# A hybrid encoder block on one core: one more seven-product pair of k-tiles in ten blocks, an eighth load place, new step lists

## The chip, the core and the metric

The kernel runs on one core of one Trainium2 chip. The metric is the device time of one execution in microseconds (us); less is better. The core's engines are TensorE (PE, with PEld for its weight loads), VectorE (DVE), ScalarE (ACT), GpSimd (POOL) and SyncE (SP); SP issues nearly all loads, POOL issues those that add to what is in place.

## The reference

One layer of an encoder block on 256 tokens of width 2048, in float32. Cut to what matters here:

```
proj = rms_norm(x) @ w_in            # q/k/v of mixers A and B, q of C, three gates
merged = sum over A, B, C of  sigmoid(gate_i) * (mixer_i @ w_br_i)
x = x + merged @ w_o                 # 2048 x 2048
hf = rms_norm(x) @ w_ffn_in          # 2048 x 11264
x = x + (silu(hf[:, :5632]) * hf[:, 5632:]) @ w_ffn_out
```

Nearly all of the time is these matrix products: 256 rows of activations by weights that are read once.

## The kernel before, in words

**Products.** Each float32 operand is split into a high part and the rest, both in the format that TensorE reads at full rate. For a weight tile ACT writes the high part (`whi`, line 395) and DVE subtracts it to get the rest (`wlo`, line 405). A product of two tiles is then three matmuls: high by high, high by rest, rest by high. All of them are issued at line 77.

**Blocks.** From `merging` on (line 816) the work is a row of blocks. A block makes 256 tokens by two neighbouring groups of 512 output columns, over 16 k-tiles of 128 (12 in the last two blocks), taken two at a time as a pair `u`. `pair` (line 407) makes one block, by a list of steps written out by hand (the `STEPS` strings, lines 54 to 61). The list says for each pair whether it takes eight products or seven:

- `d` and `D`: a whole pair for the first and the second column group, four products each. So a pair in the plain way costs eight products (24 matmuls) and two loads, each split once.
- `f`, `g`, `h`, `p`, `q`: a pair by Strassen's scheme in Winograd's form, with seven products (21 matmuls). `fetch_both` (line 479) loads both column groups into two places, `b1` and `b2`, and has POOL issue a third load that adds the first group's first half to `b2` (line 483). `f` (`first`) splits `b1`: two products. `g` (`second`) makes the sums s2 and s3 on DVE (lines 504 and 505), splits `b2`: two products. `h` (`third`) makes the fourth sum, s2 + b1 (line 523), splits it: one product. `p` and `q` (`rest`) split s2 and s3 of two pairs at a time: one product for each pair. The activations' sums that the scheme needs, the forms, are made by `sums_of` (line 796) and `token_sums` (line 787).

In the lists, `h1` serves all seven-product pairs from 1 up to the next `h`. Two fourth sums stay in the two `b1` places until the `h` step, which splits them as two halves of 512 columns, by two instructions on ACT and two on DVE.

**What sets the order.** The steps of all blocks form one chain. `run` (line 576) lets the splits go up to four steps ahead of the products. Instructions on TensorE and SP keep the program's order, and so do the splits and sums on ACT and DVE that go through `follow`; the rest (the ends of blocks, transposes, gates) is placed between them. `whi` and `wlo` have four buffers each and a fifth for every fifth step (`halves`, line 385).

**Places.** Loads go into places (`free`, line 199; `load`, line 205), taken from the front of a list and put back at its end once split: six from the start and a seventh after the attention part (line 782). `pair` fetches a seven-product pair up to four steps before its `f` if more than four places are free, else at `f` itself (lines 560 to 564). A load into a place waits until the place's last reader is done, and SP's later loads stand behind it.

**The blocks in order.** The gate and branch blocks of `merging` (one gate block by `STEPS_GATE`, four by `STEPS`, branch products between them), two blocks by `w_o` (`STEPS_O`), then eleven blocks by `w_ffn_in` (the first by `STEPS_FFN`, the others by `STEPS_IN`) with, after the 4th, the 8th and the last, two blocks by `w_ffn_out` (`STEPS_OUT` and `STEPS_OUT2`, at the end twice `STEPS_LAST`).

Of the kernel before, what the change touches and what calls it, by code (L numbers as in the profile page):

```python
# [18 lines left out]
P = 128  # L19
# [31 lines left out]

STEPS = "d0 D0 f1 d4 g1 D4 f2 d5 g2 D5 h1 f3 d6 g3 h3 p0 p2 D6 q0 q2 d7 D7".split()
STEPS_GATE = "d0 D0 d4 D4 f1 d5 g1 D5 f2 g2 d6 h1 f3 g3 h3 p0 p2 D6 q0 q2 d7 D7".split()
STEPS_IN = "d0 D0 f1 d5 g1 D5 f2 g2 h1 f3 d6 g3 f4 g4 h3 p0 p2 D6 q0 q2 d7 D7".split()
STEPS_FFN = "d0 D0 d1 D1 d4 D4 f2 d5 g2 D5 f3 d6 g3 h2 p0 D6 q0 d7 D7".split()
STEPS_O = "d0 D0 d1 D1 f2 d4 g2 D4 f3 d5 g3 D5 h2 d6 p0 D6 q0 d7 D7".split()
STEPS_OUT = "d0 D0 d1 D1 d2 D2 f6 d3 g6 D3 f7 d4 g7 h6 p0 D4 q0 d5 D5".split()
STEPS_LAST = "d0 D0 f2 d1 g2 D1 f3 d4 g3 h2 p0 D4 q0 d5 D5".split()  # L60
STEPS_OUT2 = "d0 D0 f5 d1 g5 D1 f6 d2 g6 D2 h5 f7 d3 g7 h7 p0 p2 D3 q0 q2 d4 D4".split()


class InOrder:
# [37 lines left out]
def encoder_block(ctx: ExitStack, tc: tile.TileContext, a: dict, out: bass.AP):  # L102
# [93 lines left out]
            tick()  # L196

    spare = []
    free, place_of = [(rp, f"raw{i}") for i in range(6)], {}

    def release(raw):

# [204 lines left out]
    def pair(src, lhs, order, done, forms=None, operand=None, parts=None):  # L407
# [92 lines left out]
        def second(u):  # L500
            def ready():
                b1, b2 = held[u]
                s2, s3 = t2[:, those.index(u)], t3[:, those.index(u)]
                nc.follow(nc.vector.tensor_add(s2, b2[:, 0], b2[:, 1]))
                nc.follow(nc.vector.tensor_sub(s3, s2, b1[:, 0]))
                hi, lo = halves(b2)
                release(b2)

                def products():
                    mul("W", forms(u, 0), hi[:, 0], lo[:, 0])  # L510
                    mul("Z", forms(u, 2), hi[:, 1], lo[:, 1])
                    if left["W"] == 0:
                        copy(("B", 1), "W")
                return products
            return ready

        def third(u):
            us = [v for v in those if u <= v and not any(u < w <= v for w in fourths)]

            def ready():  # L520
                low_ones = [held.pop(v)[0] for v in us]
                for v, b1 in zip(us, low_ones):
                    nc.follow(nc.vector.tensor_add(b1[:, 1], t2[:, those.index(v)], b1[:, 1]))
                hi, lo = halves(*(b1[:, 1] for b1 in low_ones))
                for b1 in low_ones:
                    release(b1)

                def products():
                    for i, v in enumerate(us):
                        mul("V", at(2 * v + 1, 1), hi[:, i], lo[:, i])  # L530
                return products
            return ready
# [279 lines left out]
    def form_room(n, pool=None):  # L812
        tiles = [s8([P, 2, 2, 4, P], "forms", pool=pool) for _ in range((n + 1) // 2)]
        return [tiles[i // 2][:, i % 2] for i in range(2 * len(tiles))]

    def merging():
        forms = sums_of(xT, (1, 2, 3), form_room(3, tail))
        for b, (g0, k0, k1) in enumerate(((0, 0, 2), (8, 2, 6), (4, 6, 12))):
            for j in (0, 2) if b else (2,):
                sg = [None, None]  # L820

                def gates(c, r, sg=sg):
                    sg[c] = r
                    for t in range(T):
                        nc.scalar.activation(r[:, t], r[:, t], AF.Sigmoid, scale=r_x[:, 0, t:t + 1])

                def merge(c, r, j=j, b=b, sg=sg):
                    n0 = (j + c) * NC
                    for t in range(T):
                        nc.vector.tensor_mul(sg[c][:, t] if b else mg[t][:, n0:n0 + NC], r[t], sg[c][:, t])  # L830

                    def later():
                        yield 1
                        for t in range(T):
                            m = mg[t][:, n0:n0 + NC]
                            nc.vector.tensor_add(m, m, sg[c][:, t])
                        if b == 2:
                            to = s8([P, 2, 4, S], "mT", pool=tail)
                            mT.append(to)
                            yield 2  # L840
                            yield from transposed([mg[t][:, n0:n0 + NC] for t in range(T)],
                                                  lambda k, n: (to[:, 0, k:k + n], to[:, 1, k:k + n]))
                    if b:
                        start(urgent(later()))

                yield pair(block_pair(a["w_gate"], g0 + j), xT, STEPS if b else STEPS_GATE, gates, forms)
                yield pair(lambda u, c, j=j, k0=k0: a["w_br"][j + c][k0 // PK + u], lambda k, k0=k0: ol(k0 + k),
                           whole_k((k1 - k0) // 2), merge)

# [4 lines left out]
    def projecting():  # L854
# [2 lines left out]
            nc.sync.dma_start(out=x[t], in_=a["x"][t * P:(t + 1) * P, :])  # L857
        x1T.extend(s8([P, 2, 4, S], "x1T") for _ in range(4))
        mTl = lambda k: (mT[k // 4][:, 0, k % 4], mT[k // 4][:, 1, k % 4])
        oforms = sums_of(mTl, (2, 3), form_room(2))  # L860
        for n in (0, 2):
            def add(c, r, n=n):
                xc = [x[t][:, (n + c) * NC:(n + c + 1) * NC] for t in range(T)]
                for t in range(T):
                    nc.vector.tensor_add(xc[t], r[:, t], xc[t])

                def later():
                    yield 1
                    sq = s4([P, T, NC], "sq")
                    for t in range(T):  # L870
                        nc.scalar.activation(sq[:, t], xc[t], AF.Square, accum_out=ss1[:, t, n + c:n + c + 1])
                    yield 2
                    yield from transposed(xc, lambda k, m: (x1T[n + c][:, 0, k], x1T[n + c][:, 1, k]),
                                          lambda k: gT[:, 2, 4 * (n + c) + k:4 * (n + c) + k + 1], 2)
                    if n + c == 1:
                        room.extend(form_room(4) + [spare[0].tile([P, 2, 4, P], F32R, name="form")])
                        forms.append(by_pair((1, 2, 3, 4), room[:4]))
                        sums_of(x1l, (1, 2, 3), room[:3])
                    elif n + c == 2:
                        sums_of(x1l, (4,), room[3:4])  # L880
                    elif n + c == 3:
                        yield 2
                        ssr = small.tile([P, T], F32, name="ss", bufs=1)
                        nc.vector.tensor_reduce(ssr, ss1, axis=AX.X, op=ALU.add)
                        row_scale(ssr, r_f)
                start(urgent(later()))
            yield pair(block_pair(a["w_o"], n), mTl, STEPS_O, add, oforms)

# [5 lines left out]
    def feeding():  # L894
        for c0, c1 in ((0, 4), (4, 8), (8, KF // 4)):
# [25 lines left out]
                yield pair(lambda u, c, n=n: a["w_ffn"][n][2 * u + c], x1l, STEPS_IN if n else STEPS_FFN, hidden,  # L921
                           lambda u, f: forms[0](u, f))
            if last:
                pairs = STEPS_LAST, STEPS_LAST
                out_forms = by_pair((2, 3), late)
            else:
                pairs = STEPS_OUT, STEPS_OUT2
                sums_of(hTl, (5,), room[4:])
# [111 lines left out]
```

## Time and profile before

| | before |
|---|---|
| median of 3 runs | 1371.34 us (1371.25 to 1371.46) |
| the profiled execution's own time | 1371.87 us |
| its span, first to last instruction | 1370.0 us |
| TensorE clock granted | 1.000 |
| DVE busy | 1165.8 us (85%) |
| ACT busy | 848.6 us (62%) |
| POOL busy | 78.1 us (6%) |
| loads of a pair added to by POOL | 75 |

The profile page has the busy time of each engine, the span in 40 slices, and the chain of work that ended last, followed back from the end. The view of waits lists for each engine what it waited for: us in total, times, the longest. The windows view gives busy time by engine in chosen stretches, with the number of instructions in brackets.

### The profile page before, as it was taken

To read this page: it belongs to the slowest core of one execution; us is meant where nothing else is said; L and a number is where in the kernel's file an instruction comes from. 1 tells how busy PE (TensorE), PEld (TensorE's weight loads), DVE (VectorE), ACT (ScalarE), POOL (GpSimd) and SP (SyncE) were. 2 spreads that over 40 slices of the span, in tenths; PEclk is the share of its full clock that TensorE was granted. 3 is DMA by queue.
4 is the path that set the end of the run, shared out by engine and by line. 5 is a ranking of instruction groups with operands and counts; after the bars stand their busy time and mean duration, and the time that the engine had idled before them with its cause. 6 is when DMAs were issued, how large, how long until landed. Compare 5 with 4: busy or idle time off the path is not lost.

```text
span 1370.0 us, 17909 instructions
## 1 busy us (share of the span) xinstructions
PE 1362.6 (99%) x6219; PEld 1129.1 (82%) x6219; DVE 1165.8 (85%) x1646; ACT 848.6 (62%) x1158; POOL 78.1 (6%) x89
## 2 busy tenths in 40 slices
PE   9999999999999999999999999999999999999998
PEld 7888888888888888888888888887888888888887
DVE  6868877758878878878989998989899988999997
ACT  7777666646665564656666666555566664566663
POOL 0010000000000000000000000000010000010000
PEclk9999999999999999999999999999999999999999
DMA  9876455557776776765767776777787767677773
GB/s 367 328 241 204 144 160 161 175 172 226 211 240 194 213 238 196 275 195 177 221 200 238 228 220 200 218 238 213 215 244 224 230 202 229 209 236 230 224 223 109
DMA packets 90524, 296.78 MB, mean 217 GB/s; under 512 B 10241, under 2 KB 12801, under 8 KB 90177
## 3 DMA queue, kind: packets, MB, share of 16 engines
q1 hardware_dynamic: 79488, 275.94, 59.9%
q0 software_dynamic: 10800, 19.67, 8.7%
q8 instruction: 49, 0.80, 0.2%
q14 instruction: 43, 0.34, 0.1%
q10 hardware_dynamic: 144, 0.02, 0.0%
HBM read 292.71 MB, written 2.88 MB: 216 GB/s over the span
## 4 chain that ended last, share of the span: by engine, by line
PE 95%; DVE 3%; DMA 1%; issue 0%; ACT 0%; SPq 0%; DVEq 0%; ACTq 0%
PE mm L77 16%; PE mmZ L77 16%; PE mmV L77 16%; PE mmY L77 16%; PE mmQ L77 13%; PE mmX L77 11%; PE mmW L77 3%; DVE wlo L405 1%; PE tp L77 1%; PE sc L77 1%; PE o L77 1%; DMA raw<-in_w_ffn 1%; PE pT L77 1%; PE hT L77 0%; DMA raw<-in_w_mem 0%
## 5 line engine op out<-in xcount | busy, mean ns | idle before, releaser
L395 ACT ACTIVATE whi<-raw 128x1024 fp32r<-128x1024 f32 (+1 forms) x490 | 479.4, 991 | 370.2 <-PE mmV L77 98.3
L405 DVE TENSOR_TENSOR wlo<-raw,whi 128x1024 fp32r<-128x1024 f32 (+1 forms) x490 | 549.4, 1137 | 99.2 <-ACT whi L395 94.9
L77 PE MATMUL mm<-whi,xT 128*128 128x512 f32 x640 | 203.0, 393 | 0.0
L77 PEld LDWEIGHTS mm<-whi,xT 128*128 128x128 f32 x640 | 119.2, 188 | 24.3 <-issue 1.1
L131 DVE TENSOR_TENSOR wlo<-raw,whi 128x1024 fp32r<-128x1024 f32 x82 | 101.8, 1245 | 40.3 <-ACT whi L130 39.8
L77 PE MATMUL mm<-wlo,xT 128*128 128x512 f32 x320 | 125.3, 392 | 0.0
L130 ACT ACTIVATE whi<-raw 128x1024 fp32r<-128x1024 f32 x82 | 86.7, 1061 | 61.8 <-PE mm L77 45.7
L405 DVE TENSOR_TENSOR wlo<-t,whi 128x1024 fp32r<-128x1024 f32 x82 | 90.0, 1130 | 20.2 <-ACT whi L395 20.1
L77 PE MATMUL mmX<-whi,forms 128*128 128x512 f32 x292 | 97.7, 389 | 0.0
L77 PE MATMUL mmY<-whi,x1T 128*128 128x512 f32 x268 | 95.8, 393 | 0.0
L395 ACT ACTIVATE whi<-t 128x1024 fp32r<-128x1024 f32 x82 | 78.5, 981 | 25.8 <-PE mmV L77 15.8
L77 PE MATMUL mmV<-whi,x1T 128*128 128x512 f32 x268 | 93.4, 389 | 0.0
L77 PEld LDWEIGHTS mm<-wlo,xT 128*128 128x128 f32 x320 | 60.2, 188 | 11.6
L77 PE MATMUL mmZ<-whi,x1T 128*128 128x512 f32 x184 | 65.1, 395 | 0.0
L77 PE MATMUL mmQ<-whi,x1T 128*128 128x512 f32 x184 | 64.3, 390 | 0.0
L77 PEld LDWEIGHTS mmX<-whi,forms 128*128 128x128 f32 x292 | 54.8, 188 | 11.4
L483 POOL DMA_DIRECT2D raw<-in_w_ffn x42 | 36.3, 864 | 449.1 <-DVE wlo L405 200.5
L77 PEld LDWEIGHTS mmY<-whi,x1T 128*128 128x128 f32 x268 | 50.3, 188 | 10.5 <-ACT whi L395 0.4
L77 PEld LDWEIGHTS mmV<-whi,x1T 128*128 128x128 f32 x268 | 50.3, 188 | 10.5
L77 PE MATMUL mmW<-whi,forms 128*128 128x512 f32 x146 | 56.9, 390 | 0.0
L77 PE MATMUL mmZ<-whi,forms 128*128 128x512 f32 x146 | 56.9, 389 | 0.0
L77 PE MATMUL mmX<-wlo,forms 128*128 128x512 f32 x146 | 56.8, 389 | 0.0
(284 smaller groups left out, 2835.8 us busy)
## 6 DMA issues: line engine op xcount, KB each, us to landing
raw<-in_w_ffn SPq DMA_DIRECT2D x176, 512.0 KB, 4.9
raw<-in_w_gate SPq DMA_DIRECT2D x96, 512.0 KB, 4.5
raw<-in_w_ffn_out SPq DMA_DIRECT2D x88, 512.0 KB, 4.5
raw<-in_w_qkv SPq DMA_DIRECT2D x64, 512.0 KB, 4.4
raw<-in_w_o SPq DMA_DIRECT2D x32, 512.0 KB, 4.9
raw<-in_w_br SPq DMA_DIRECT2D x24, 512.0 KB, 4.7
raw<-in_w_ffn POOLq DMA_DIRECT2D x42, 256.0 KB, 6.4
raw<-in_w_mem SPq DMA_DIRECT2D x15, 512.0 KB, 7.9
```

Of the source, the lines that this page charges most:

```text
L77: ins = op(*args, **kw)
L130: nc.scalar.activation(hi, src, AF.Copy)
L131: nc.vector.tensor_sub(lo, src, hi.bitcast(F32))
L395: nc.follow(nc.scalar.activation(hi[:, o], v, AF.Copy))
L405: nc.follow(nc.vector.tensor_sub(*due.pop(0)))
L483: nc.gpsimd.dma_start(out=b2[:, 0], in_=src(u, 0)[:, :NC], accum_op=ALU.add)
```

## The change

Every block list is new. Counting the `f` letters, ten blocks get one more seven-product pair: the four gate blocks that went by `STEPS` and now go by `STEPS_IN` (3 to 4), the two `w_o` blocks (2 to 3), the first `w_ffn_in` block (2 to 3), the first of the two `w_ffn_out` blocks in the first two groups (2 to 3), and the very last block, by the new `STEPS_LAST2` (2 to 3). In the other blocks only the order of the steps changes. There is a seventh place from the start, so eight later; the memory comes from the room of POOL's DMA descriptors, halved to 4096 bytes. The fourth sum of every second pair is now made at its `g` step, into the half of the pair before it that is no longer needed, so that its own `b1` place is free at once, and `h` splits both sums by one instruction of 1024 columns. Three more forms are made: pair 4 of the gates' input, pair 1 of `merged`, pair 1 of the last hidden group.

```diff
-STEPS = "d0 D0 f1 d4 g1 D4 f2 d5 g2 D5 h1 f3 d6 g3 h3 p0 p2 D6 q0 q2 d7 D7".split()
-STEPS_GATE = "d0 D0 d4 D4 f1 d5 g1 D5 f2 g2 d6 h1 f3 g3 h3 p0 p2 D6 q0 q2 d7 D7".split()
-STEPS_IN = "d0 D0 f1 d5 g1 D5 f2 g2 h1 f3 d6 g3 f4 g4 h3 p0 p2 D6 q0 q2 d7 D7".split()
-STEPS_FFN = "d0 D0 d1 D1 d4 D4 f2 d5 g2 D5 f3 d6 g3 h2 p0 D6 q0 d7 D7".split()
-STEPS_O = "d0 D0 d1 D1 f2 d4 g2 D4 f3 d5 g3 D5 h2 d6 p0 D6 q0 d7 D7".split()
-STEPS_OUT = "d0 D0 d1 D1 d2 D2 f6 d3 g6 D3 f7 d4 g7 h6 p0 D4 q0 d5 D5".split()
-STEPS_LAST = "d0 D0 f2 d1 g2 D1 f3 d4 g3 h2 p0 D4 q0 d5 D5".split()
-STEPS_OUT2 = "d0 D0 f5 d1 g5 D1 f6 d2 g6 D2 h5 f7 d3 g7 h7 p0 p2 D3 q0 q2 d4 D4".split()
+STEPS_GATE = "d4 d0 D0 f1 g1 d5 D5 f2 d6 g2 D4 f3 h1 g3 p0 p2 D6 q0 h3 q2 d7 D7".split()
+STEPS_IN = "d0 D0 f1 d5 D5 g1 f2 g2 d6 h1 f3 f4 g3 D6 g4 p0 p2 h3 q0 q2 d7 D7".split()
+STEPS_O = "f1 d0 D0 g1 d4 d5 f2 g2 D4 h1 f3 g3 p0 p2 d6 h3 D6 q0 q2 D5 d7 D7".split()
+STEPS_FFN = "d1 d0 D0 f2 g2 D1 f3 f4 d5 D5 g4 g3 p0 h2 d6 p2 h4 D6 q0 q2 d7 D7".split()
+STEPS_OUT = "d3 d2 d1 f5 d0 D2 D1 f6 D0 g5 f7 D3 g6 g7 p0 p2 h5 q0 q2 h7 d4 D4".split()
+STEPS_OUT2 = "d1 d2 d0 f5 D0 D2 g5 f6 f7 g6 g7 p0 d3 p2 D1 h5 h7 q0 D3 q2 d4 D4".split()
+STEPS_LAST = "d1 d0 D0 D1 f2 g2 d4 D4 f3 g3 p0 h2 q0 d5 D5".split()
+STEPS_LAST2 = "d4 f1 d0 D4 g1 f2 f3 D0 g2 g3 p0 h1 p2 h3 q0 q2 d5 D5".split()
...
-    free, place_of = [(rp, f"raw{i}") for i in range(6)], {}
+    free, place_of = [(rp, f"raw{i}") for i in range(7)], {}
...
                 hi, lo = halves(b2)
                 release(b2)
+                if u not in fourths:
+
+                    before = held[those[those.index(u) - 1]][0]
+                    nc.follow(nc.vector.tensor_add(before[:, 0], s2, b1[:, 1]))
+                    release(held.pop(u)[0])
...
         def third(u):
-            us = [v for v in those if u <= v and not any(u < w <= v for w in fourths)]
+            us = [v for v in those[those.index(u):][:2] if v == u or v not in fourths]
 
             def ready():
-                low_ones = [held.pop(v)[0] for v in us]
-                for v, b1 in zip(us, low_ones):
-                    nc.follow(nc.vector.tensor_add(b1[:, 1], t2[:, those.index(v)], b1[:, 1]))
-                hi, lo = halves(*(b1[:, 1] for b1 in low_ones))
-                for b1 in low_ones:
-                    release(b1)
+                b1 = held.pop(u)[0]
+                nc.follow(nc.vector.tensor_add(b1[:, 1], t2[:, those.index(u)], b1[:, 1]))
+                hi, lo = halves(b1 if len(us) > 1 else b1[:, 1])
+                release(b1)
 
                 def products():
-                    for i, v in enumerate(us):
+                    for i, v in enumerate(reversed(us)):
                         mul("V", at(2 * v + 1, 1), hi[:, i], lo[:, i])
...
     def merging():
-        forms = sums_of(xT, (1, 2, 3), form_room(3, tail))
+        forms = sums_of(xT, (1, 2, 3, 4), form_room(4, tail))
...
-                yield pair(block_pair(a["w_gate"], g0 + j), xT, STEPS if b else STEPS_GATE, gates, forms)
+                yield pair(block_pair(a["w_gate"], g0 + j), xT, STEPS_IN if b else STEPS_GATE, gates, forms)
...
-        oforms = sums_of(mTl, (2, 3), form_room(2))
+        oforms = sums_of(mTl, (1, 2, 3), [form()] + form_room(2))
...
-                pairs = STEPS_LAST, STEPS_LAST
-                out_forms = by_pair((2, 3), late)
+                pairs = STEPS_LAST, STEPS_LAST2
+                sums_of(hTl, (1,), room[4:])
+                out_forms = by_pair((1, 2, 3), room[4:] + late)
...
-    nc = _bacc.Bacc("TRN2", target_bir_lowering=False, num_devices=1, dynamic_dma_scratch_size=8192)
+    nc = _bacc.Bacc("TRN2", target_bir_lowering=False, num_devices=1, dynamic_dma_scratch_size=4096)
```

More of the change, by code (lines that the diff above doesn't have):

```diff
@@ L814, in form_room @@
         return [tiles[i // 2][:, i % 2] for i in range(2 * len(tiles))]
+    form = lambda: spare[0].tile([P, 2, 4, P], F32R, name="form")
     def merging():
-        forms = sums_of(xT, (1, 2, 3), form_room(3, tail))
+        forms = sums_of(xT, (1, 2, 3, 4), form_room(4, tail))
         for b, (g0, k0, k1) in enumerate(((0, 0, 2), (8, 2, 6), (4, 6, 12))):
@@ L875, in later @@
                     if n + c == 1:
-                        room.extend(form_room(4) + [spare[0].tile([P, 2, 4, P], F32R, name="form")])
+                        room.extend(form_room(4) + [form()])
                         forms.append(by_pair((1, 2, 3, 4), room[:4]))
```

## The prediction, made before the changed kernel ran

> **What bounds the kernel now.** I read the page first: busy time, granted clock and the chain that ended last.
>
> ```profile
> span 1370.0 us, 17909 instructions
> PE 1362.6 (99%) x6219; PEld 1129.1 (82%) x6219; DVE 1165.8 (85%) x1646; ACT 848.6 (62%) x1158; POOL 78.1 (6%) x89
> PE   9999999999999999999999999999999999999998
> PEclk9999999999999999999999999999999999999999
> PE 95%; DVE 3%; DMA 1%; issue 0%; ACT 0%; SPq 0%; DVEq 0%; ACTq 0%
> ```
>
> TensorE is busy for all but 7.4 us, at full clock, and 95% of the chain is its own work. Busy alone proves little where matmuls overlap, so the second view is the chain piece by piece, for the pace of one matmul, and the third is what PE itself waited for.
>
> ```profile
> 743.25 2.72 PE mmX L77 x12
> PE mmY L77 <- DVE wlo L405: 1.2, 3, 0.8
> PE mmW L77 <- DVE wlo L405: 0.4, 2, 0.2
> PE mmZ L77 <- DVE wlo L405: 0.3, 1, 0.3
> ```
>
> Twelve matmuls take 2.72 us back to back: 0.2267 us each. In the whole span PE's recorded waits for split weights come to 1.9 us. So the time is the number of matmuls times their pace, as long as DVE delivers. The fourth view asks how near DVE is to failing: the windows of single blocks, cut from one block's first matmul to the next one's. In order: the `STEPS_GATE` block, the first and the last of the four `STEPS` blocks, the two `w_o` blocks, the first and second `w_ffn_in` blocks, the first `STEPS_OUT` block, the fifth and sixth `w_ffn_in` blocks, the last block.
>
> ```profile
> 313.49:354.97 41.48, 41.48 (x185) 34.35 (x183) 38.23 (x51) 26.71 (x33) 2.57 (x3) 1.00 0.71 221
> 360.41:401.89 41.48, 41.48 (x185) 34.35 (x183) 33.23 (x37) 24.79 (x29) 1.71 (x2) 1.00 0.68 207
> 522.93:566.32 43.39, 43.39 (x200) 35.93 (x199) 38.97 (x54) 26.50 (x33) 0.86 (x1) 1.00 0.64 210
> 582.64:626.74 44.10, 44.10 (x204) 36.49 (x203) 34.51 (x40) 24.64 (x30) 1.73 (x2) 1.00 0.65 198
> 626.74:670.83 44.09, 44.09 (x204) 36.49 (x202) 41.04 (x63) 29.34 (x43) 0.86 (x1) 1.00 0.65 202
> 670.83:714.92 44.09, 44.09 (x203) 36.49 (x202) 38.79 (x67) 29.95 (x42) 2.59 (x3) 1.00 0.66 208
> 714.92:756.69 41.77, 41.77 (x190) 34.57 (x188) 39.15 (x46) 27.47 (x33) 3.45 (x4) 1.00 0.73 227
> 840.22:883.35 43.13, 43.13 (x196) 35.70 (x194) 35.77 (x46) 25.07 (x30) 2.59 (x3) 1.00 0.69 212
> 924.83:967.42 42.59, 41.62 (x181) 33.63 (x180) 39.60 (x48) 23.84 (x29) 3.45 (x4) 1.00 0.74 221
> 967.42:1009.73 42.31, 42.10 (x190) 34.42 (x188) 38.73 (x46) 28.32 (x35) 3.45 (x4) 1.00 0.73 222
> 1334.46:1370.03 35.57, 31.44 (x139) 25.71 (x137) 26.37 (x34) 13.72 (x16) 0.00 (x0) 1.00 0.33 111
> ```
>
> The columns are the block's length, then busy time and count of PE, PEld, DVE, ACT and POOL. The second `w_ffn_in` block already has four seven-product pairs and DVE busy for 39.15 of 41.77 us, and still PE never stops: such a block can run at PE's pace. Counted by hand it holds 4 x 24 + 4 x 21 = 180 matmuls, 40.81 us, and the 0.96 us left are the transposes. The fifth and sixth blocks of the same list take 42.59 and 42.31 us: 0.82 and 0.54 us of waiting. I found no other late block.
>
> **Term 1: the matmuls.** A pair in the plain way is eight products of three matmuls, in the new way seven. Ten blocks get one more such pair: 10 x 3 x 0.2267 = 6.80 us less on the engine that sets the end. All added work is on other engines. The Trainium skill, page "TensorE: Matmul & The Clock Gate", section "Back-to-back issue gap", gives 518 cycles of 2.4 GHz, 216 ns, for a matmul of 512 columns; by it the term would be 6.5 us. The trace has 227 ns, and that is used.
>
> **Term 2: the splits and sums that pay for it.** The chain through the one late spot shows each operation at the pace at which DVE and ACT do them in a row, and the load that comes late.
>
> ```profile
> 932.62 0.61 DVE t L504
> ...
> 933.26 0.69 DVE t L505
> 933.95 1.14 DVE wlo L405
> 935.09 1.20 DVE raw L523 x2
> 936.29 1.15 DVE wlo L405
> ...
> 937.45 5.32 DMA raw<-in_w_ffn
> ...
> 942.88 1.07 ACT whi L395
> ```
>
> A plain pair costs DVE two splits, 2 x 1.14 = 2.28 us. A seven-product pair costs `f` and `g` 2.28, half a split for `h` (0.57), half for `p` and half for `q` (1.14), and three sums of 0.61 (1.83): 5.82 us. So each swap adds 3.5 us to DVE, up to 3.7 where a lone half is split by itself at 0.60. Since the block also gets 0.68 us shorter, DVE must find 4.2 us of idle time in it. ACT pays 1.5 splits, 1.6 us, and has over 14 us idle in each of these blocks.
>
> Length less DVE busy gives that idle time: 8.3 us in the first `STEPS` block, 4.4 in the last of them, 9.6 and 3.05 in the `w_o` blocks, 5.3 in the first `w_ffn_in` block, 7.4 in the `STEPS_OUT` block, 9.2 in the last. Only the second `w_o` block is short, by some 1.1 us; it also makes the next block's forms. What covers a shortage is the lead of the splits:
>
> ```profile
> ACT whi L395 <- PE mmV L77: 114.1, 91, 1.7
> ```
>
> ACT stood 91 times, 114.1 us in all, waiting for a matmul to give back a `whi` buffer, which means that all buffers were full. A block so enters with several steps in hand, each worth 1.36 us of matmuls (two products) or 2.72 (four). A debt of 1.1 us fits in, if the lead is not spent elsewhere. Without that cover it is paid in full.
>
> The three added forms cost DVE, by the rows below, two sums of 0.418, one of 0.419, two of 0.284 (line 793 is as large as line 792) and the split of 0.686: 2.5 us each.
>
> ```profile
> L802 DVE TENSOR_TENSOR ffull<-xT x6: 418/418/419, 310.5 to 317.0; 128x256 f32<-128x256 f32 x6
> L791 DVE TENSOR_TENSOR fraw<-ffull x17: 416/419/427, 311.3 to 1280.2; 128x256 f32<-128x256 f32 x17
> L792 DVE TENSOR_TENSOR fraw<-fraw,ffull x17: 280/284/294, 312.3 to 1283.5; 128x128 f32<-128x128 f32 x17
> L131 DVE TENSOR_TENSOR forms<-fraw,forms 128x512 fp32r<-128x512 f32 x15 | 10.3, 686 | 0.4 <-ACT forms L130 0.4
> ```
>
> One falls in the `STEPS_GATE` block, idle 3.25 us, which gets no new pair: 0.8 left. One falls ahead of the first `w_o` block or in it: 9.6 less 4.2 less 2.5 leaves 2.9. The last lies where the last two blocks have room. Splitting two fourth sums at once gives back 1.20 - 1.14 = 0.06 us of DVE for each double `h`; I count it as nothing.
>
> So I book 0.6 us of new PE waits, between 0 (the lead covers all) and 3 us. The upper end is 1.1 in the second `w_o` block, as much again in the first `w_ffn_in` block, which would inherit no lead, and 0.8 in the gate blocks, two of which have under 1 us of idle DVE left.
>
> **Term 3: the places.** The same chain tells why the fifth `w_ffn_in` block is late. The load that lands at 942.8 starts at 937.45, the moment the split that frees its place ends. That is `d6`, and counting the list of places by hand it gets the place of `g2`, only 4.08 us of matmuls before it (`g2`, `h1`, `f3`, 1.36 each). Before `g2`'s split could end, DVE had first to do the two sums of `h1`, 1.20 us. In the new list `d6` gets the place of `g1`, again 4.08 us before (`g1`, `f2`, `g2`), so the eighth place by itself buys this load nothing. But no sums stand between `g1`'s sums and its split, and two plain steps, each of which gains 2.72 - 1.14 = 1.58 us of lead, now stand between `f1` and `g1`, where one stood between `g1` and `f2`. That is 1.2 us and more, against waits of 0.82 and 0.54. I book 1.1 of the 1.36 us as gained (between 0 and 1.36).
>
> Counted the same way, every other plain load finds its place freed at least 8.2 us of matmuls before its use, against the 5.32 + 1.07 + 1.14 = 7.5 us of load and split. The pairs are fetched earlier in the `STEPS_IN` list: `f3` and `f4` 9.5 and 10.9 us before their `g`, where it was 5.4 and 6.8. They come later at `f7` of `STEPS_OUT` (at its own step, 5.4 us before) and `f1` of `STEPS_O` (at its own step, 6.8); see the third rival. The moved fourth sum is the same 0.61 us, on DVE ahead of the split of `g2` or `g4`; who waits for that are two products of a step that now has `D6` before `g4`. The halved room of POOL's descriptors I cost at nothing: at most four pairs are fetched in a block of 41 us. The same goes for the seventh place in the part before `merging`, where PE is full in every slice of the page.
>
> **Sum.** -6.8 + 0.6 - 1.1 = -7.3 us. On the profiled execution (1371.87 us, of which 1370.0 are span) that gives 1364.6; it ran 0.53 over the median of the runs, 1371.34, on which I forecast 1364.0. The last 4.1 us, in which PE is idle in the last block, stay: that list still ends in `d5 D5`.
>
> **The rivals.** A difference of 0.2%, 2.74 us, is about what a measurement of this kernel can tell from no change: 1368.6 and 1374.1 are the bounds.
>
> *DVE runs dry.* The debt is paid at its upper end and nothing is gained at the places: 1371.34 - 6.8 + 3 = 1367.5. For it: DVE 93% busy in the second `w_o` block. Against: the buffers that were full 91 times. 13%.
>
> *PE was never the bound.* Then fewer matmuls only lengthen its pauses, and the time stays at 1371.3. For it: PEld at 82%. Against: in the second `w_ffn_in` block PEld is at 34.57 of 41.77, 83%, while a matmul starts every 0.2267 us without a gap. The Trainium skill, page "Perfetto Trace Analysis", section "Identifying the Most-Contended Engine", says that matmul busy is a poor measure and that weight-load busy tells the headroom; by it 18% would be free and term 1 would be worth nothing. This trace differs: 83% is a full PE here. 5%, and 2% for mixtures that come to rest within 0.2%.
>
> *The added fetch comes too late (slower).* Place: `f7` in both `STEPS_OUT` blocks, `f1` in both `STEPS_O` blocks.
>
> ```profile
> raw<-in_w_ffn_out SPq DMA_DIRECT2D x88, 512.0 KB, 4.5
> raw<-in_w_ffn_out POOLq DMA_DIRECT2D x14, 256.0 KB, 6.5
> L483 POOL DMA_DIRECT2D raw<-in_w_ffn x42: 862/862/881, 657.9 to 1270.8; - x42
> ```
>
> From the free place to the split `b2` it is 4.5 + 0.86 + 6.5, two sums (1.3), and 1.07 + 1.14: 15.4 us. If SP issues the loads no earlier than the step itself, 15.4 - 5.4 = 10 us must come out of a lead of four steps, at most 5.4 to 10.9 us. With 5 us exposed at four sites the time is 1371.3 - 6.8 + 20 = 1384.5; it turns slower from 2.4 us at each site on. Against: SP issues a load as soon as its place is free, and by the list `b2` of `f7` gets the place of `d0`, freed 19 us of matmuls before `g7`, and `b2` of `f1` one freed over 28 us before. 5%.
>
> *POOL held up by DVE (slower).* Each of the ten added POOL issues waits out a DVE operation of up to 1.14 us with nothing to hide it: 1371.3 - 6.8 + 11.4 = 1375.9. Against: 42 POOL issues last 862 to 881 ns while DVE is busy 94% of the time in such blocks; none is stretched. The Trainium skill, page "SBUF — State Buffer", section "SBUF: two separate sides", says that GpSimd and a DVE operation in a two-port mode shut each other out, so that descriptors wait; the POOL row does not show it. 3%.
>
> **How the numbers follow.** The forecast's own case, 72%, spans 1363.2 (no new wait, 1.36 gained) to about 1366.5. With DVE running dry, 13%, faster is 85%. The range goes from 1362.9 to 1367.8, which takes in both ends of terms 2 and 3 and the first rival; what lies outside is the same and slower cases and a little more. Same is 5% + 2%, slower 5% + 3%.
>
> **What would show it.** Right: about 30 fewer matmuls; 85 POOL loads; lengths of the changed blocks 0.68 us less (40.8 for the first gate block of the four, 43.4 for the `w_o` blocks); the fifth and sixth `w_ffn_in` blocks at 41.8; DVE busy up by some 40 us to over 1200; PE's waits for `wlo` under 2 us. Wrong: waits of PE for `wlo` in the second `w_o` block or the two blocks after it above 3 us; a load or a POOL load that ended last ahead of `g7` or `g1`; a `w_ffn_in` block longer than 41.8 in every group.

## The result and the profile after

The changed kernel is slower: 1384.03 us, the median of 4 runs (1382.84 to 1385.41), beside 1371.4 us for the kernel before in the same job (4 runs, 1371.25 to 1372.89). The ratio is 1.0090, with a 95% interval from 1.0073 to 1.0107. The profiled execution took 1382.84 us, its span 1381.1. The prediction had 1364.0 us and a range up to 1367.8.

Four lines of the page of the changed kernel: the work is as forecast.

```profile
span 1381.1 us, 17893 instructions
...
PE 1361.9 (99%) x6189; PEld 1127.6 (82%) x6189; DVE 1203.1 (87%) x1678; ACT 867.0 (63%) x1145; POOL 87.0 (6%) x99
...
PE   9999999999999999997989999999999999999998
...
L483 POOL DMA_DIRECT2D raw<-in_w_ffn x43 | 37.3, 867 | 447.1 <-DMA raw<-in_w_ffn 195.5
```

There are 30 matmuls fewer, DVE has 37.3 us more work, and POOL's loads still take 867 ns each. But PE's row, which was 9 in every slice but the last, shows 7, 9, 8 at slices 19 to 21. PE's busy time hides the size of it: it fell by 0.7 us where 6.8 were removed, since matmuls at half clock count as busy for longer. The windows of blocks show where. In order: the first gate block of the four, the two `w_o` blocks, the first, fifth and sixth `w_ffn_in` blocks, the last block (length, then busy time and count of PE, PEld, DVE, ACT, POOL; then PE's clock).

```profile
360.75:401.55 40.80, 40.80 (x182) 33.78 (x180) 37.02 (x41) 26.70 (x29) 2.55 (x3) 1.00 0.73 225
580.36:623.75 43.39, 43.39 (x201) 35.92 (x199) 38.06 (x47) 26.26 (x32) 2.15 (x3) 1.00 0.69 203
623.75:679.17 55.42, 47.43 (x201) 38.09 (x199) 44.36 (x66) 30.66 (x43) 3.04 (x4) 0.94 0.58 175
679.17:729.23 50.06, 45.66 (x201) 37.07 (x199) 42.20 (x70) 31.16 (x45) 1.73 (x2) 0.97 0.60 180
938.48:979.28 40.80, 40.80 (x181) 33.78 (x180) 39.23 (x44) 25.51 (x28) 3.45 (x4) 1.00 0.76 225
979.28:1021.05 41.77, 41.77 (x190) 34.58 (x188) 38.97 (x45) 26.99 (x30) 3.46 (x4) 1.00 0.76 231
1345.46:1381.07 35.61, 31.08 (x136) 25.08 (x134) 30.72 (x40) 15.35 (x18) 0.00 (x0) 1.00 0.34 107
```

Two blocks carry the whole loss. The second `w_o` block takes 55.42 us instead of 44.09, the first `w_ffn_in` block 50.06 instead of 44.09: +11.33 and +5.97. The other blocks gained or stayed: the first `w_o` block is 0.70 us shorter, the fifth and sixth `w_ffn_in` blocks 1.79 and 0.54, four gate blocks and two `w_ffn_out` blocks 0.58 to 0.68 each. The last two blocks and the start are 0.75 us longer together. The sum is +11.1 us, the difference of the spans. PE's waits name what it stood for:

```profile
PE mmW L77 <- DVE x1T L134: 4.2, 1, 4.2
PE tp L77 <- DVE x1T L134: 3.6, 1, 3.6
PE mmZ L77 <- DVE x1T L134: 2.7, 1, 2.7
PE tp L77 <- DVE x L870: 1.8, 2, 1.3
...
PE mmZ L77 <- DVE wlo L405: 0.8, 1, 0.8
```

Splits (`wlo`), the danger that the prediction weighed, are at 0.8 us. The new name is `x1T`: the transposed `x`, the input of the `w_ffn_in` blocks. Each `w_o` block makes two blocks of 512 columns of `x`, and `transposed` (line 280) turns them on TensorE into the tiles `tp`, while the next block already runs. It works in two halves for each block of `x` (lines 283 to 286; what empties `tp` follows them):

```python
        for h in range(2):
            if h:
                yield lag
            tp = bank("tp", "mm" if h and nc.on else "at")
```

A `tp` lies in a PSUM bank until ACT and DVE have emptied it, by two instructions each, since every 128 columns have a gain of their own. Lines 115 and 124 give the name `at` four banks and the name `mm` four. In `mul` (line 432) the accumulators X, Y and Z come from `at`, V, Q and W from `mm`. So each side has four banks for three accumulators and for the two `tp` of its half. X and W belong to the `f` and `g` steps alone: X is opened by the first `f`, W by the first `g`.

Now the timeline of PE in the second `w_o` block, before (start, duration; each `tp` row is one group of four transposes; rows between them left out):

```profile
629.46 0.60 PE L77 MATMUL tp<-ident,x 128*128 128x128 f32 x4
...
639.06 0.60 PE L77 MATMUL tp<-ident,x 128*128 128x128 f32 x4
639.41 0.48 PE L77 MATMUL mmX<-whi,mT 128*128 128x512 f32 x1
...
643.63 0.39 PE L77 MATMUL mmW<-whi,forms 128*128 128x512 f32 x1
```

All four groups (629.46 to 639.06) go before X and W are opened: on each side two accumulators and two `tp`, four banks. The same view after:

```profile
623.75 0.39 PE L77 MATMUL mmX<-whi,mT 128*128 128x512 f32 x1
...
625.88 0.55 PE L77 MATMUL tp<-ident,x 128*128 128x128 f32 x3 [0.49 <-DVE x L870]
...
630.56 0.55 PE L77 MATMUL tp<-ident,x 128*128 128x128 f32 x3 [1.26 <-DVE x L870]
633.77 0.52 PE L77 MATMUL mmZ<-whi,mT 128*128 128x512 f32 x1 [2.67 <-DVE x1T L134]
634.09 0.63 PE L77 MATMUL mmZ<-wlo,mT 128*128 128x512 f32 x1
...
638.19 0.60 PE L77 MATMUL tp<-ident,x 128*128 128x128 f32 x4
638.54 0.48 PE L77 MATMUL mmW<-whi,form 128*128 128x512 f32 x1
...
643.76 0.63 PE L77 MATMUL tp<-ident,x 128*128 128x128 f32 x4 [3.58 <-DVE x1T L134]
```

X is opened by the block's first matmul. Two groups follow, which wait for `x` itself, since the short step `f1` brings them sooner than DVE has made it. With X, Y and these two the `at` side is full, and Z, the fifth, waits 2.67 us. Then V, Q, the third group and W fill the `mm` side, and the fourth group waits 3.58 us. DVE's timeline shows why a bank stays full for so long:

```profile
630.42 0.48 DVE L134 SCALAR_TENSOR_TENSOR x1T<-tp,gT,x1T 128x256 fp32r<-128x256 f32 x1
630.82 0.68 DVE L505 TENSOR_TENSOR t<-t,raw 128x512 f32<-128x512 f32 x1
631.41 0.68 DVE L511 TENSOR_TENSOR raw<-t,raw 128x512 f32<-128x512 f32 x1
632.02 1.22 DVE L405 TENSOR_TENSOR wlo<-raw,whi 128x1024 fp32r<-128x1024 f32 x1
633.15 0.87 DVE L134 SCALAR_TENSOR_TENSOR x1T<-tp,gT,x1T 128x256 fp32r<-128x256 f32 x2
```

DVE's two instructions for the first bank start at 630.42 and 633.15; between them stand two sums and a split for later steps, 2.3 us from 630.82 on, which PE doesn't need yet. The second one ends at 633.63 (0.48 us, as the first), and Z starts 0.14 us later. Last, PE's clock in three stretches of these two blocks (the clock stands behind POOL's column):

```profile
633.70:637.20 3.50, 3.43 (x9) 2.73 (x10) 0.80 (x2) 0.47 (x1) 0.00 (x0) 0.55 0.00 0
644.10:647.70 3.60, 3.60 (x12) 2.83 (x11) 3.60 (x12) 1.79 (x4) 0.00 (x0) 0.53 0.61 236
695.60:698.80 3.20, 3.20 (x8) 2.52 (x9) 2.30 (x10) 0.43 (x2) 0.00 (x0) 0.50 0.29 109
```

Each follows a pause of PE, 2.83, 3.75 and 4.36 us, and then come some 3.4 us at half clock. A pause is counted here from one start to the next, less the usual 0.11 us behind a transpose or 0.23 us behind a matmul; the view of waits, which counts from the modelled end, has 2.7, 3.6 and 4.2. So against the 43.4 us forecast for it, the second `w_o` block's excess of 12.0 us is 0.66 + 1.42 of waiting for `x`, 2.83 + 3.75 for banks, and the 3.4 us left of slow matmuls. In the first `w_ffn_in` block, 6.7 us, the pauses come to 5.0 (4.36 and two small ones of 0.3 us), and 1.6 are left for slow matmuls.

### The profile page after: what moved, and what is told of

Its sections match the earlier page's. It is cut to its first block, busy times and chain, and to the rows that moved or that the text cites. A ratio compares the mean times of both kernels' runs of the same rounds, so it can differ in the third digit from the quotient of the medians.

```text
span 1381.1 us, 17893 instructions
## 1 busy us (share of the span) xinstructions
PE 1361.9 (99%) x6189; PEld 1127.6 (82%) x6189; DVE 1203.1 (87%) x1678; ACT 867.0 (63%) x1145; POOL 87.0 (6%) x99
## 4 chain that ended last, share of the span: by engine, by line
PE 95%; DVE 3%; DMA 1%; issue 1%; ACT 1%; SPq 0%; DVEq 0%; ACTq 0%
PE mm L77 16%; PE mmZ L77 16%; PE mmY L77 16%; PE mmV L77 16%; PE mmX L77 12%; PE mmQ L77 11%; PE mmW L77 4%; PE tp L77 1%; DVE wlo L405 1%; PE sc L77 1%; PE o L77 1%; PE pT L77 1%; PE hT L77 0%; ACT whi L395 0%; DMA raw<-in_w_mem 0%
## 5 line engine op out<-in xcount | busy, mean ns | idle before, releaser
L405 DVE TENSOR_TENSOR wlo<-t,whi 128x1024 fp32r<-128x1024 f32 x94 | 105.0, 1118 | 13.6 <-ACT whi L395 12.5
L395 ACT ACTIVATE whi<-t 128x1024 fp32r<-128x1024 f32 x94 | 91.5, 974 | 26.9 <-PE mmQ L77 11.9
L77 PE MATMUL mmX<-whi,forms 128*128 128x512 f32 x312 | 105.0, 389 | 0.0
L77 PEld LDWEIGHTS mmX<-whi,forms 128*128 128x128 f32 x312 | 58.6, 188 | 12.2
L77 PE MATMUL mmW<-whi,forms 128*128 128x512 f32 x156 | 62.2, 398 | 4.2 <-DVE x1T L134 4.2
L483 POOL DMA_DIRECT2D raw<-in_w_ffn x43 | 37.3, 867 | 447.1 <-DMA raw<-in_w_ffn 195.5
L77 PE MATMUL mmZ<-whi,forms 128*128 128x512 f32 x156 | 61.3, 393 | 0.0
L77 PE MATMUL mmX<-wlo,forms 128*128 128x512 f32 x156 | 60.7, 389 | 0.0
L505 DVE TENSOR_TENSOR t<-t,raw 128x512 f32<-128x512 f32 x85 | 58.4, 686 | 1.6
```

The source lines that it names most:

```text
L77: ins = op(*args, **kw)
L395: nc.follow(nc.scalar.activation(hi[:, o], v, AF.Copy))
L405: nc.follow(nc.vector.tensor_sub(*due.pop(0)))
L483: nc.gpsimd.dma_start(out=b2[:, 0], in_=src(u, 0)[:, :NC], accum_op=ALU.add)
```

## The experiments

My theory was the count of banks: a list that opens its third accumulator of a side before the transposes of `x` have left their banks makes PE wait. The rival was load: with a third seven-product pair DVE has too little time in these two blocks. A third theory came up with the first runs: DVE comes over the border of two blocks behind, with `x` not yet made. The table gives the three blocks' lengths, from the same kind of window as above, each from one profiled execution, and the ratio to the kernel before, whose median was 1372.5 to 1373.6 us in the jobs of the experiments (a dash: one execution only).

| kernel | ratio (95% interval) | first `w_o` | second `w_o` | first `w_ffn_in` |
|---|---|---|---|---|
| before | 1 | 44.09 | 44.09 | 44.09 |
| changed | 1.0090 (1.0073 to 1.0107) | 43.39 | 55.42 | 50.06 |
| e1_plain_first | 1.0022 (1.0013 to 1.0032) | 47.51 | 43.43 | 51.92 |
| e2_old_f_first | 1.0095 (1.0078 to 1.0112) | 44.64 | 54.59 | 44.12 |
| e3_no_gain | - | 43.39 | 49.53 | 45.16 |
| e4_old_two_lists | 0.9955 (0.9941 to 0.9970) | 44.09 | 44.09 | 44.09 |
| e5_old_list_wo | - | 44.09 | 44.09 | 49.59 |
| e6_old_list_ffn | - | 43.39 | 56.11 | 44.09 |
| e7_x_later | 1.0039 (1.0024 to 1.0054) | 43.41 | 49.86 | 50.45 |
| e10_wo_first_only | 0.9958 (0.9941 to 0.9974) | 43.39 | 44.09 | 44.09 |
| e11_ffn_plain_first | 0.9977 (0.9967 to 0.9986) | 43.39 | 44.09 | 46.45 |
| e13_three_ahead | 1.0067 (1.0049 to 1.0085) | 45.24 | 54.78 | 47.21 |
| e14_spread | 1.0002 (0.9993 to 1.0011) | 43.39 | 45.43 | 49.23 |
| e17_spread_g4_late | 0.9955 (0.9939 to 0.9971) | 43.39 | 45.43 | 43.41 |
| e18_wo_plain_first | 0.9979 (0.9969 to 0.9988) | 43.39 | 43.43 | 48.81 |
| e19_spread_d6_early | 0.9958 (0.9944 to 0.9972) | 43.39 | 43.60 | 44.61 |

### Order or load

The kernel before, with an `f` and a `g` early in its `w_o` list and no work added:

```diff
-STEPS_O = "d0 D0 d1 D1 f2 d4 g2 D4 f3 d5 g3 D5 h2 d6 p0 D6 q0 d7 D7".split()
+STEPS_O = "f2 d0 D0 g2 d1 d4 f3 D1 D4 g3 d5 D5 h2 d6 p0 D6 q0 d7 D7".split()
```

> The kernel before with one list changed, that of the w_o blocks, to f2 d0 D0 g2 d1 d4 f3 ...: still two seven-product pairs, no work added anywhere, but X opens at the first step and W at the fourth. Bank theory: the second w_o block gets the waits of the changed kernel, there 12 us, so 1371.3 + 8 to 12 = 1379 to 1383. Load theory: no work is added, 1371 to 1372.

The second `w_o` block took 54.59 us, and PE's waits were those of the changed kernel:

```profile
PE tp L77 <- DVE x1T L134: 4.2, 1, 4.2
PE mmZ L77 <- DVE x1T L134: 2.2, 1, 2.2
```

The order alone makes 10.5 us of loss (54.59 for 44.09) where the changed kernel has 12.0, so most of it needs no added load. (The kernel came to 1384.58 us, 1.6 over the upper end of what was expected.) The other way round, the changed kernel with lists that begin with plain steps and keep the third seven-product pair:

```diff
-STEPS_O = "f1 d0 D0 g1 d4 d5 f2 g2 D4 h1 f3 g3 p0 p2 d6 h3 D6 q0 q2 D5 d7 D7".split()
+STEPS_O = "d0 D0 d4 D4 f1 d5 g1 D5 f2 g2 d6 h1 f3 g3 h3 p0 p2 D6 q0 q2 d7 D7".split()
-STEPS_FFN = "d1 d0 D0 f2 g2 D1 f3 f4 d5 D5 g4 g3 p0 h2 d6 p2 h4 D6 q0 q2 d7 D7".split()
+STEPS_FFN = "d0 D0 d1 D1 f2 d5 g2 D5 f3 g3 d6 h2 f4 g4 h4 p0 p2 D6 q0 q2 d7 D7".split()
```

> The changed kernel with other lists for the w_o blocks (d0 D0 d4 D4 f1 d5 g1 D5 ...) and the first w_ffn_in block (d0 D0 d1 D1 f2 d5 g2 D5 ...): the same number of seven-product pairs, so the same work on every engine, but four plain steps ahead of the first f and six steps ahead of the first g. Bank theory (the accumulators X and W are opened while the transposes of the block before still hold banks, and PE then waits for VectorE to empty one): the 18.7 us of excess in the second w_o block and the first w_ffn_in block go, 1384.0 - 18.7 = 1365, between 1364 and 1367. Load theory (VectorE has 3.5 us too much to do in these two blocks): nothing is taken off VectorE, so the excess stays, 1376 or more.

The second `w_o` block came to 43.43 us, what the prediction had for it, with the added work in it. But the two others got worse for reasons of their own: in the first `w_o` block `d4` came before its input was there (PE waited 2.1 us for `mT`), and in the first `w_ffn_in` block PE waited 2.5 us for `x` and 1.9 us for the part of `x1T` that `d5` reads. So the total, 1375.86 us, is neither what the bank theory gave nor, by a little, what the load theory gave.

### Whose list

The changed kernel with both lists of before, with the old `w_o` list alone, with the old `w_ffn_in` list alone, and with the new `w_o` list in the first `w_o` block only (there what is transposed is `merged`, which has no gain and leaves a bank by one instruction on each engine):

```diff
-STEPS_O = "f1 d0 D0 g1 d4 d5 f2 g2 D4 h1 f3 g3 p0 p2 d6 h3 D6 q0 q2 D5 d7 D7".split()
+STEPS_O = "d0 D0 d1 D1 f2 d4 g2 D4 f3 d5 g3 D5 h2 d6 p0 D6 q0 d7 D7".split()
-STEPS_FFN = "d1 d0 D0 f2 g2 D1 f3 f4 d5 D5 g4 g3 p0 h2 d6 p2 h4 D6 q0 q2 d7 D7".split()
+STEPS_FFN = "d0 D0 d1 D1 d4 D4 f2 d5 g2 D5 f3 d6 g3 h2 p0 D6 q0 d7 D7".split()
```

> The changed kernel with the lists of before for the w_o blocks and the first w_ffn_in block, so seven swaps instead of ten and three times 0.68 us of matmuls more. Bank theory: 1365 + 2.0 = 1367. Load theory: the same, 1367, since VectorE's added work goes from these blocks too. If the time stays over 1374, neither is right and the loss sits elsewhere.

The first two of these four lines alone, and the last two alone:

> The changed kernel with the w_o list of before; the new w_ffn_in list stays. If the loss of each list is made inside the block that uses it (accumulators of the list opened while the transposes of x still hold their banks), both w_o blocks take 44.1 us and the first w_ffn_in block keeps its loss, about 50 us: some 1371 to 1373 us in all, 1366.3 (both old lists) and 5 to 6.6. If the first w_ffn_in block was late because VectorE came out of the w_o blocks behind, its loss goes with theirs: about 44 us there, and 1365 to 1366.5 in all.

> The changed kernel with the w_ffn_in list of before; the new w_o list stays. If the loss is made inside the block by its own list, the second w_o block keeps 55 us and the first w_ffn_in block takes 44 to 45: about 1377 us in all (1366.3 and 11, less 0.68 for the first w_o block). If VectorE's debt is carried over the border, the first w_ffn_in block is still 2 us or more late with its old list: 1379 us or more.

And all four, with the new list kept as `STEPS_O0` for the first `w_o` block and the old one as `STEPS_O2`:

```diff
-            yield pair(block_pair(a["w_o"], n), mTl, STEPS_O, add, oforms)
+            yield pair(block_pair(a["w_o"], n), mTl, STEPS_O2 if n else STEPS_O0, add, oforms)
```

> The changed kernel with the new w_o list in the first w_o block alone, where what is transposed is emptied by one operation a bank, and the lists of before in the second w_o block and in the w_ffn_in blocks. If a new list harms only where transposes of x, with four operations a pair of banks, are pending: first w_o block 43.4 us, second 44.1, first w_ffn_in block 44.1, 1365.6 us in all (1366.3 less 0.68). If the new list leaves a debt of VectorE work behind, the second w_o block is late by 1 us or more: over 1366.6.

With both old lists the kernel is faster than before, 0.9955. Each new list makes its loss in its own block: 49.59 us in the first `w_ffn_in` block with only that list new, 56.11 in the second `w_o` block with only the other, and 44.09 in the neighbour each time. Nothing is carried over the border here. The new list in the first `w_o` block alone takes 43.39 us and leaves no debt; its 0.70 us is too little for the ratio to show.

### Banks

First, `x` without its gain, so that a bank is emptied by one instruction on ACT and one on DVE:

```diff
-                    yield from transposed(xc, lambda k, m: (x1T[n + c][:, 0, k], x1T[n + c][:, 1, k]),
-                                          lambda k: gT[:, 2, 4 * (n + c) + k:4 * (n + c) + k + 1], 2)
+                    yield from transposed(xc, lambda k, m: (x1T[n + c][:, 0, k:k + m], x1T[n + c][:, 1, k:k + m]), lag=2)
```

> The changed kernel with its lists, but each transpose of x is emptied by one split of 512 columns without the channel gain (0.58 + 0.69 us) instead of two of 256 with it (twice 0.46 + 0.48 us); this leaves the multiplication by g_ffn out. Bank theory: a bank comes free after one turn of ScalarE and VectorE instead of two, so about half of the waits go, 1374 to 1380. Load theory: only 1.2 us of VectorE's work per block goes, 1382 or more.

The excess fell from 12.0 to 6.1 us and from 6.7 to 1.8, by half and by more than half. The one execution took 1370.98 us, below what either theory gave. The direction fits the banks, but the edit also takes work off DVE and ACT. So next, nothing is left out, and only the transposes in the second `w_o` block come four steps later:

```diff
-                    yield 2
+                    yield 2 if n else 6
```

> The changed kernel with both new lists; only the transposes of x in the first w_o block are made four steps later, when f1, g1 and g2 have opened their accumulators; no instruction is added or left out. If the order of accumulators and transposes makes the loss, the second w_o block comes down from 55.4 us to 43.4 to 46, and the first w_ffn_in block, whose transposes are not touched, stays at about 50: 1372 to 1375 us. If too little VectorE time is left in the block, it stays at 55 and the kernel at 1383 to 1385.

The block came to 49.86 us: the wait of Z is gone, and the first `w_ffn_in` block, which wasn't touched, stays at 50.45. But I had expected 46 at most. The timeline of PE shows what I had not counted to the end:

```profile
634.84 0.60 PE L77 MATMUL tp<-ident,x 128*128 128x128 f32 x4
...
639.30 0.63 PE L77 MATMUL tp<-ident,x 128*128 128x128 f32 x4 [1.11 <-DVE x1T L134]
...
641.15 0.60 PE L77 MATMUL tp<-ident,x 128*128 128x128 f32 x4
...
646.51 1.09 PE L77 MATMUL tp<-ident,x 128*128 128x128 f32 x4 [3.37 <-DVE x1T L134]
```

With three accumulators open a side has one bank left. The second group of each side (639.30 and 646.51) waits until the first has been emptied. Before testing that, another reading of the queues had to be tried: that the emptying is late because it stands behind a split that itself waits for PE's buffer. One step less of lead takes that split away:

```diff
-    run(everything(), 4)
+    run(everything(), 3)
```

> The changed kernel with both new lists; the splits are issued three steps ahead of the products instead of four, nothing else. If the emptying of the transposes' banks is late because it stands on the queues of ScalarE and VectorE behind a split that needs the buffer PE is just reading, one step less ahead takes that split from in front of it: the second w_o block comes down from 55.4 us to 44 to 50 and the first w_ffn_in block from 50.1 to 44 to 47, 1370 to 1378 us if the other blocks stay within 1 us. If VectorE has too little time in those two blocks, less lead can only make them longer: 1384 us or more.

It fell for the second `w_o` block: 54.78 us, with the same two waits. (The first `w_ffn_in` block came down to 47.21, near what that reading had, but its wait only moved, to X, and the first `w_o` block now waited 1.6 us for `mT`.)

```profile
PE tp L77 <- DVE x1T L134: 3.3, 1, 3.3
PE mmZ L77 <- DVE x1T L134: 2.7, 1, 2.7
```

So the count was put to the test: the two groups of a side far apart, by a delay of the second block of `x`.

```diff
-                    yield 2
+                    yield 3 + 4 * c
```

> The changed kernel with both new lists and all its added work; only the four groups of transposes of x in each of the three blocks that make them are placed anew: the first block's of a pair one step later, the second block's five steps later. Counted on four banks for X, Y, Z and a first half and four for V, Q, W and a second half: with the three accumulators of a side open one bank is left, so that a group waits until the last group of its side is emptied, which took 5 to 8 us. Placed like this, two groups of a side lie some ten microseconds apart. If the banks are the cause: second w_o block 43.4 to 44.5 us instead of 55.4, first w_ffn_in block 43.4 to 44.5 instead of 50.1, PE's waits for x1T under 1 us, and 1363.5 to 1366 us in all (in a job with before at 1371.4; by ratio 0.994 to 0.996), the prediction's own number. If VectorE's load in those two blocks is the cause, which stays the same to the instruction: 1378 us or more.

(The blocks that make these transposes are two, the second `w_o` block and the first `w_ffn_in` block.)

PE's longest waits, then:

```profile
PE mmW L77 <- ACT forms L130: 2.1, 1, 2.1
PE mmX L77 <- ACT SA L446: 1.7, 1, 1.7
PE mmW L77 <- DVE forms L131: 1.7, 1, 1.7
```

Not one wait for `x1T` or `x` is left, in either block, with all of the added work in place. The second `w_o` block gave back 10.0 of 12.0 us. The total missed what I expected all the same, 1.0002: in the first `w_ffn_in` block the forms of pair 4, which are made after the transposes, now came too late for `g4`, and in the second `w_o` block X waited for its copy to `SA`. Whether these two were the load after all was open. Two edits of the order, the second on top of the first, told:

```diff
-STEPS_FFN = "d1 d0 D0 f2 g2 D1 f3 f4 d5 D5 g4 g3 p0 h2 d6 p2 h4 D6 q0 q2 d7 D7".split()
+STEPS_FFN = "d1 d0 D0 f2 g2 D1 f3 f4 d5 D5 g3 d6 g4 p0 h2 p2 h4 D6 q0 q2 d7 D7".split()
-STEPS_O = "f1 d0 D0 g1 d4 d5 f2 g2 D4 h1 f3 g3 p0 p2 d6 h3 D6 q0 q2 D5 d7 D7".split()
+STEPS_O = "f1 d0 D0 g1 d4 d5 f2 g2 D4 h1 f3 g3 d6 p0 p2 h3 D6 q0 q2 D5 d7 D7".split()
```

> The changed kernel with the transposes placed as in e14_spread, and in the w_ffn_in list g4 two steps later (g3, d6, g4 instead of g4, g3). If the banks made the block's loss and the late forms of the fourth pair only took their place: first w_ffn_in block 43.4 to 45 us instead of 49.2, 1366.5 to 1369 us in all (in a job with before at 1371.4; by ratio 0.9965 to 0.998), the second w_o block at 45.4 as in e14_spread. If VectorE's load makes it, another wait takes the place again: 47 us or more, and 1371 us or more.

> As e17_spread_g4_late, and in the w_o list d6 two steps earlier, between g3 and p0. If the last loss of the second w_o block is only X waiting for the copy that is issued too shortly before it: 43.4 to 43.8 us there instead of 45.4, and 0.9935 to 0.9945 of before, 1363 to 1364.5 us beside 1371.4. If ScalarE and VectorE are short of time in this block, the wait moves to another instruction: 44.5 us or more, 0.995 or more.

With the first edit the first `w_ffn_in` block takes 43.41 us, the very length that term 1 gives it. With the second the second `w_o` block takes 43.60. The windows of these two blocks in the last kernel:

```profile
623.33:666.93 43.60, 43.60 (x201) 35.84 (x199) 42.41 (x65) 30.30 (x43) 3.45 (x4) 1.00 0.73 223
666.93:711.53 44.60, 43.70 (x200) 35.85 (x199) 42.56 (x71) 31.27 (x45) 1.89 (x3) 1.00 0.68 204
```

DVE is busy for 42.41 of 43.60 us, 97%, and PE doesn't stop once: the load rival falls here, as it did in the first `w_ffn_in` block with the 43.41 us of e17. There 0.9 us of waiting for the forms came back in e19, and the block takes 44.61: the forms of pair 4 come so close to their use that little decides, and what delayed them here was not tried. The ratio was expected at 0.9945 at most and is 0.9958; its interval reaches 0.9944.

### Plain steps first, and the border

Two more lists with three seven-product pairs open X and W after the transposes, without moving these: in the second `w_o` block (e18) and in the first `w_ffn_in` block (e11), each on top of e10.

```diff
+STEPS_O2 = "d0 D0 d4 D4 f1 d5 g1 D5 f2 g2 d6 h1 f3 g3 h3 p0 p2 D6 q0 q2 d7 D7".split()
```

```diff
+STEPS_FFN = "d0 D0 d1 D1 d5 D5 f2 d6 g2 f3 g3 h2 f4 D6 g4 p0 p2 h4 q0 q2 d7 D7".split()
```

> The changed kernel with its w_o list in the first w_o block, in the second a list with the same three seven-product pairs that starts with four plain steps, and the w_ffn_in list of before. If three sevens cost nothing once X is opened at the fifth step and W at the seventh, after the transposes of x: w_o blocks 43.4 us each, first w_ffn_in block 44.1 to 44.5, 0.9937 to 0.995 of before (about 1363.5 us beside 1371.4). If the third seven leaves VectorE behind at the border, the first w_ffn_in block waits for x by 1.5 us or more: 0.9955 to 0.997.

> The changed kernel with the new w_o list in the first w_o block, the list of before in the second, and a w_ffn_in list with the third seven-product pair of k-tiles that starts with six plain steps, so that the third accumulator is opened at its seventh step. If a third seven does no harm once its accumulators are opened after the transposes of x have gone: first w_ffn_in block 43.4 us instead of 44.1, 1365 to 1365.6 us (in one job with before at 1371.4; by ratio 0.9955 to 0.9965). If the third seven itself costs VectorE time that the block doesn't have, or d5 comes before its x is transposed: 45 us or more.

The `w_o` block runs at 43.43 us, but the block after it is 48.81 instead of 44.09:

```profile
PE tp L78 <- DVE x L871: 2.7, 2, 2.5
```

Here is the debt over the border: DVE works without a break through the end of the `w_o` block (648 to 674 us), the sum that makes the `x` waited for starts only at 672.11, and a transpose due at 670.1, which holds PE's order, stops PE for 2.74 us; then the clock is at half (0.51 from 673.90 to 677.30). In the other kernel `d5` came before its `x1T` (1.4 us, and 0.4 more): 46.45 us, the second of the two outcomes that I had written down.

### The place alone

The kernel before with seven places from the start and half the descriptor room, nothing else:

```diff
-    free, place_of = [(rp, f"raw{i}") for i in range(6)], {}
+    free, place_of = [(rp, f"raw{i}") for i in range(7)], {}
-    nc = _bacc.Bacc("TRN2", target_bir_lowering=False, num_devices=1, dynamic_dma_scratch_size=8192)
+    nc = _bacc.Bacc("TRN2", target_bir_lowering=False, num_devices=1, dynamic_dma_scratch_size=4096)
```

> The kernel before with the eighth place for loads and nothing else. If the place alone brings the sixth loads of the fifth and sixth w_ffn_in blocks no earlier (the prediction's third term, which gives their gain to the new order), those blocks stay at 42.6 and 42.3 us and the kernel within 0.3 us of before. If a place was what they lacked: 40.8 to 41.8 us each and 1369.0 to 1370.3 us, with other blocks unchanged.

It took 0.9978 of before (0.9969 to 0.9988). The fifth and sixth `w_ffn_in` blocks:

```profile
925.17:965.97 40.80, 40.80 (x181) 33.78 (x180) 39.72 (x48) 26.14 (x30) 3.45 (x4) 1.00 0.79 236
965.97:1007.74 41.77, 41.77 (x190) 34.58 (x188) 39.35 (x46) 27.57 (x33) 3.48 (x4) 1.00 0.79 228
```

They are as short as in the changed kernel. The place alone does it.

## Why the prediction was wrong

**Term 1, the matmuls, was right.** Seven of the ten blocks got shorter by 0.58 to 0.70 us, and the first `w_ffn_in` block and the second `w_o` block reach 43.41 and 43.60 us once nothing holds them up. The last block is the exception: 35.61 us after 35.57. Nearly all of the 0.68 us saved there went to one stop, where X waits for its copy to `SB` (0.3 us in the view of waits, 0.6 from start to start). The tail behind the last matmul is 4.2 us, where it was 4.1; what sets it was not tried.

**Term 2 is the step that failed**: "So I book 0.6 us of new PE waits, between 0 (the lead covers all) and 3 us." The measured waits and slow matmuls of these two blocks, the second `w_o` block and the first `w_ffn_in` block, come to 18.7 us. The load that the term counted was sized well (DVE +37.3 us, where some 40 were forecast), and e19 shows that the idle time was enough even in the block that I called short by 1.1 us. What failed is the assumption that idle time of DVE and a lead of splits are all that PE needs from DVE. PE also needs banks back, and their emptying doesn't profit from the lead: it stands in DVE's queue among the splits of later steps. I read the new lists for when a load and a split come, and not for when an accumulator opens, though the lists state that in their first letter. In the trace of before it could be seen: four groups of `tp`, and X only behind the last of them, in the `w_o` block and in the `w_ffn_in` block alike.

**Term 3 had the right blocks and the wrong cause.** I wrote that "the eighth place by itself buys this load nothing" and gave the gain to the order. The place alone brings both blocks to their full pace. The size was low too: 2.33 us against 1.1, with a bound of 1.36, because I measured both blocks against 41.77 us, the length of the second block. That fits the sixth. The fifth makes no transposes (181 instructions on PE, not 190) and takes 40.80 us at full pace, so it had lost 1.79 us and not 0.82.

**The rivals.** *DVE runs dry* had the engine but not the mechanism: e2 makes most of the loss without the load, and e17 and e19 carry the load without the loss. *PE was never the bound* is refuted by the blocks that got shorter at the forecast pace; weight loads at 83% were a full PE again. *The added fetch comes too late* did not happen: both `STEPS_OUT` blocks are 0.68 us shorter, and the first `w_o` block 0.70. *POOL held up by DVE* did not either: 867 ns for each load. None of the cases of the slower side was the one that came, and the chance of 8% for all of them was too small for a change that writes eight orders anew.

**What stays open.** The sum of the terms with the banks put right would be near the forecast, but e19 comes to a span of 1363.9 us, 6.1 under before and not 7.3: the last two blocks give back 0.7 us of what the third term gained, and the first `w_ffn_in` block 1.2. The four kernels at 0.9955 to 0.9958 (e4, e10, e17, e19) beat both kernels and cannot be told from each other by these runs.

## What to carry to other kernels

When steps are put in a new order, count for each moment not only loads and buffers but the PSUM banks: the accumulators that are open, and the transposes that wait to be emptied. An instruction that empties a bank is as late as its place in its engine's queue, so an engine with idle time can still hold up TensorE for microseconds; open an accumulator after the transposes that share its banks have gone, or set those apart. Where the block lengths before and after are laid side by side, two blocks that lose much are found at once beneath many that gain little.

## What the runs showed of the hardware

A pause can cost TensorE twice. After pauses of 2.83, 3.75 and 4.36 us the matmuls of the changed kernel started every 0.427 us instead of every 0.227, for some 3.4 us; that is 5.0 (3.4 and 1.6) of the 18.7 us that the two blocks lost. The Trainium skill, page "TensorE: Matmul & The Clock Gate", section "What's actually happening", gives a window of 3413 ns, half rate after an idle window and full rate after a busy one; the length of the slow stretch agrees. But pauses shorter than such a window were enough here: in e13 one of 2.05 us brought half clock,

```profile
692.20:695.40 3.20, 3.20 (x11) 2.38 (x10) 2.98 (x9) 1.89 (x3) 0.00 (x0) 0.50 0.03 9
```

while after one of 1.89 us in e14 the clock stayed at 1.00. No limit can be read off between the two: after a pause of 2.39 us in e2, which ends at 636.68, the clock stayed at 1.00 too (636.70 to 640.00). What decides beside the length was not tried.
